# State space mixer of a two-layer diffusion backbone: where the decay masks are applied, and how the state products are formed

## The chip, the cores and the metric

One core of one Trainium2 chip runs the whole kernel. The metric is device microseconds of one execution, median over runs. TensorE (PE in the profile; its weight loads are PEld) multiplies matrices into PSUM, VectorE (DVE) and GpSimd (POOL) do elementwise work, ScalarE (ACT) does activations and copies, and DMA queues are issued from SyncE (SP) and from ScalarE. GpSimd does not touch PSUM in this kernel.

## The reference, cut to what matters

512 latent tokens and 256 context tokens of width 1024 go through two layers. Layer 0 is a gated linear attention mixer beside neighbourhood attention, layer 1 the state space mixer; after each comes a mixture of 16 experts. In layer 1 the context serves only as the start of the states. The mixer has 8 groups of 4 heads of 64 channels, a state of 128, and runs in both directions:

```python
def ssd_chunked(x, dt, a, bm, cm, h0):
    acum = jnp.cumsum(dtc * a, axis=2)
    seg = acum[:, :, :, None] - acum[:, :, None, :]
    decay = jnp.exp(jnp.where(causal, seg, -jnp.inf))
    cb = jnp.einsum('nblgk,nbsgk->nblsg', cc, bc)
    y_diag = jnp.einsum('nblsgh,nbsghp->nblghp', cb[..., None] * decay * dtc[:, :, None], xc)
    w_end = jnp.exp(acum[:, :, -1:] - acum) * dtc
    def step(hs, xs):
        y = y_d + jnp.einsum('blgk,bghpk->blghp', c_i, hs) * jnp.exp(a_i)[..., None]
        hs = exp(a_i[:, -1]) * hs + jnp.einsum('blgk,blghp->bghpk', b_i, x_i * w_i[..., None])
        return hs, y
```

The outputs of the two directions are added, then `dsk * x`, the gate silu(z), an RMS norm per group and the output projection follow. The kernel works with chunks of 128 positions instead of 64, which gives the same sums.

## The kernel before, in words

All of it is one function, `tile_backbone_kernel`. A scheduler takes the program in its written order, simulates it, and fixes for each engine and queue one order in which its instructions run; an engine that waits holds up all that stands behind it. So work of the next group is mixed into that of the present one on each engine.

The mixer starts at L1376. A first projection gives dt (64 rows: 2 directions by 32 heads). L1417 to L1476 make from it, per direction, the running sum of the decay `ac` within each chunk, `ad = ac - ln(dt)`, and the weights to a chunk's end; `ac` is stored to the DRAM tensor `acd`, and `ac`, `ad` and the weights are transposed on TensorE into `acT`, `adT` and `weT`.

Then a loop over the 8 groups (L1517). In one group: projections of x, B and C by `gemm_fm` (L825, float32 weights and inputs split into two parts, three matrix products each; `load_split` at L726 loads and splits, ScalarE casting and VectorE subtracting at L721, L722); a convolution of five taps on ScalarE and VectorE (L1482 to L1497, its running sum is `acc`); transpositions of x and B (L1545 to L1555, copied by ScalarE into `xk`, `bk`); C·B for four chunks in one PSUM bank of the `at` tag (L1556), which VectorE multiplies by a mask of ones and zeros per direction into `cb` (L1563); x weighted to the chunk's end on GpSimd (`xw`, L1572) and from it the states `st` of both directions, chunk by chunk (L1575 to L1597; GpSimd decays them, VectorE adds); the projection of z for the gate `zs` (L1598).

The part that changes is L1613 to L1651. It runs twice per group, for two halves `m` of 128 channels (two heads). A PSUM bank `o` is cleared. For each direction `d`, the two rows of `acd` are loaded on ScalarE's queue to all 128 partitions (`R`, 512 KB, two buffers). Eight VectorE instructions form `min(R, acT) - adT` in `mt` (L1627), ScalarE takes the exponential (L1629), VectorE multiplies by `cb[d]` (L1630). ScalarE takes the exponential of `R` itself (L1631) and GpSimd multiplies it by C (L1632). Then TensorE adds to the bank, per chunk and per head, x times `mt` (8 products with 64 columns of weights, 128 wide) and the chunk's state times `R` (again 8). Last, VectorE adds `dsk * x` and multiplies by the gate (L1646, L1648), ScalarE squares (L1649). The norm of a group (L1499: column sums, `rsqrt`, transposition, two products, a store to `yd`) is issued inside the next group's projections. In PSUM the tag `o` has one bank, `at` two, `tp` two and `mm` three.

After the loop, the output projection reads `yd` back (L1660), and the mixture of experts streams its weights.

The lines of the inner part that a sentence says badly:

```python
1618  for d in range(2):
1623      mt = sp.tile([128, 2, 4, 128], F32, name="mt", bufs=2)
1624      for hh in range(2):
1625          for c in range(4):
1626              h = col + hh
1627              V.tensor_scalar(mt[:, hh, c, :], R[:, hh, c, :], acT[:, c, h:h + 1], adT[:, c, h:h + 1],
1628                              op0=ALU.min, op1=ALU.subtract)
1635      def heads(c, w, r, last):
1636          for hh in range(2):
1637              mm(py[hh * 64:(hh + 1) * 64, c, :], w[:, hm][:, hh * 64:(hh + 1) * 64], r[:, hh, c, :], False, last)
1639      for c in range(4):
1640          heads(c, xk[:, c], mt, False)
1641      for n in range(4):
1642          heads(n if d == 0 else 3 - n, st[:, n, d], R, True)
```

In the trace each float32 matrix product shows as two TensorE instructions.

Of the kernel before, what the change touches and what calls it, by code (L numbers as in the profile page):

```python
# [10 lines left out]
F32 = mybir.dt.float32  # L11
# [11 lines left out]
LAT = 512  # L23
# [28 lines left out]
def kernel(ctx: ExitStack, tc: tile.TileContext, A: dict, out: bass.AP):  # L52
# [17 lines left out]
    def tp_bank(shape=None):  # L70
        return bank("tp", 2, shape)

    def at_bank(shape=None):
        return bank("at", 2, shape)

    def mm(o, l, r, start, stop, **k):
        return T.matmul(o, l, r, start=start, stop=stop, skip_group_check=True, **k)  # L77
# [1298 lines left out]
    with ExitStack() as mb:  # L1376
# [14 lines left out]
        acd = dram.tile([64, LAT], F32, name="acd")  # L1391
        lad = dram.tile([64, 4], F32, name="lad")
        with ExitStack() as sx:
            sp = sx.enter_context(tc.tile_pool(name="ssc", bufs=1, side="right"))
            tri = [sp.tile([128, 128], F32, name=f"stri{d}") for d in range(2)]
            for d in range(2):
                sgn = 1 - 2 * d
                G.memset(tri[d], 1.0)
                G.affine_select(out=tri[d], in_=tri[d], pattern=[[sgn, 128]], compare_op=ALU.is_ge, fill=0.0,
                                base=0, channel_multiplier=-sgn)  # L1400
# [7 lines left out]
            acT = sp.tile([128, NTL, 64], F32, name="acT")  # L1408
            adT = sp.tile([128, NTL, 64], F32, name="adT")
# [8 lines left out]
            e_ = sp.tile([64, TOK], F32, tag="mt", bufs=2, name="dte")  # L1418
            l_ = sp.tile([64, TOK], F32, tag="mt", bufs=2, name="dtl")
# [31 lines left out]
            V.tensor_tensor(ad, ac[:, :LAT], ad, ALU.subtract)  # L1451
# [16 lines left out]
            S.dma_start(out=acd[:, :], in_=ac[:, :LAT])  # L1468
            S.dma_start(out=eb.rearrange("p a b -> p (a b)"),
                        in_=lad.rearrange("a b -> (a b)").partition_broadcast(128))  # L1470
            S.activation(eb, eb, AF.Exp)
            for t, o, n in ((ac, acT, NTL), (ad, adT, NTL), (l_, weT, NT)):
                q = tp_bank([128, 8, 64])
                for i in range(n):
                    tr(q[:, i, :], t[:, i * 128:(i + 1) * 128])
                V.tensor_copy(o, q[:, :n, :])  # L1476
# [40 lines left out]
            for g in range(8):  # L1517
# [42 lines left out]
                cb = []  # L1560
                for d in range(2):
                    t = sp.tile([128, 4, 128], F32, name=f"cb{d}")
                    V.tensor_tensor(t, p, tri[d].unsqueeze(1).to_broadcast([128, 4, 128]), ALU.mult)  # L1563
                    cb.append(t)
# [48 lines left out]
                for m in range(2):  # L1613
                    py = bank("o", 1, [128, 4, 128])
                    clear(py)
                    hm = slice(m * 128, (m + 1) * 128)
                    for d in range(2):

                        col = d * 32 + g * 4 + m * 2
                        R = sp.tile([128, 2, 4, 128], F32, name="R", bufs=2)  # L1620
                        S.dma_start(out=R.rearrange("p h a b -> p (h a b)"),
                                    in_=acd[col:col + 2, :].rearrange("h t -> (h t)").partition_broadcast(128))
                        mt = sp.tile([128, 2, 4, 128], F32, name="mt", bufs=2)
                        for hh in range(2):
                            for c in range(4):
                                h = col + hh
                                V.tensor_scalar(mt[:, hh, c, :], R[:, hh, c, :], acT[:, c, h:h + 1], adT[:, c, h:h + 1],  # L1627
                                                op0=ALU.min, op1=ALU.subtract)
                        S.activation(mt, mt, AF.Exp)  # L1629
                        V.tensor_tensor(mt, mt, cb[d].unsqueeze(1).to_broadcast([128, 2, 4, 128]), ALU.mult)  # L1630
                        S.activation(R, R, AF.Exp)  # L1631
                        G.tensor_tensor(R, R, cT.rearrange("p (a b) -> p a b", a=4).unsqueeze(1).to_broadcast([128, 2, 4, 128]),  # L1632
                                        ALU.mult)

                        def heads(c, w, r, last):
                            for hh in range(2):
                                mm(py[hh * 64:(hh + 1) * 64, c, :], w[:, hm][:, hh * 64:(hh + 1) * 64], r[:, hh, c, :], False, last)

                        for c in range(4):
                            heads(c, xk[:, c], mt, False)  # L1640
                        for n in range(4):
                            heads(n if d == 0 else 3 - n, st[:, n, d], R, True)
                    y = sp.tile([128, LAT], F32, name="y", bufs=2)
                    sq = sp.tile([128, LAT], F32, name="ysq", bufs=2)
                    blk = g * 2 + m
                    V.scalar_tensor_tensor(y, xg[:, m, :LAT], vec("dsk", blk, 1), py.rearrange("p a b -> p (a b)"),  # L1646
                                           op0=ALU.mult, op1=ALU.add)
                    V.scalar_tensor_tensor(y, y, 0.5, zs[:, m, :], op0=ALU.mult, op1=ALU.mult)  # L1648
                    S.activation(sq, y, AF.Square)  # L1649
                    sqs.append(sq)  # L1650
                    ys.append(y)  # L1651
# [196 lines left out]
```

## Time and profile before

| | us |
|---|---|
| median of 3 runs | 2380.43 |
| lowest, highest | 2377.44, 2381.2 |
| the profiled execution, its own time | 2382.69 |
| its span, first to last instruction | 2381.0 |
| mixer's loop, from the first group's C·B product to the last group's | 1286.19 to 1753.08 |

The span is what the profile's views divide; 1.7 us of the execution lie around it. Busy time of TensorE counts overlapped instructions once, and their ends are modelled; distances between starts are the safer measure of what a stretch of matrix products costs. A group of instructions in the profile carries its line, engine, operation and tiles as output<-inputs. Matrix products are all issued in a helper at L77, so they are told apart by tiles: `o<-mt,xk` and `o<-R,st` are the heads, `at<-cT,bT` is C·B.

### The profile page before, as it was taken

The page shows a single profiled execution, that of the slowest core. Times are in us where ns is not written, and L with a number is a line of the kernel's source. Part 1 is how long each engine was busy: PE and PEld are TensorE (multiplying, and loading weights), DVE is VectorE, ACT ScalarE, POOL GpSimd, SP SyncE. Part 2 cuts the span into 40 slices and gives each one's busy share as a digit, 9 for nine tenths or more (in the row PEclk, how much of TensorE's full clock was granted, in tenths as well). Part 3 has the DMA queues.
Part 4 walks back from the last instruction along what each step waited for, and adds up shares of the span by engine and source line. Part 5 has one row for each costly group of instructions (what it writes and reads, how often), then busy time and mean ns, then how long its engine had stood idle before and what let it go on. Part 6 is the DMA issues. An engine that isn't in the chain of part 4 may idle for free. (4 is left out here: it accounts for less than half of the span.)

```text
span 2381.0 us, 37608 instructions
## 1 busy us (share of the span) xinstructions
PE 2228.0 (94%) x15522; PEld 1392.7 (58%) x15522; DVE 1273.3 (53%) x2231; ACT 847.0 (36%) x1408; POOL 513.9 (22%) x383
## 2 busy tenths in 40 slices
PE   7999999989999999999988999999989999988886
PEld 6888887877344444444476787777768633322222
DVE  5566476635243443343577888888885512222224
ACT  4446455522242343343463444434443211111111
POOL 1000044421121222221222434334442000000001
PEclk9999999999899999999998999999999899999999
DMA  8554311249999999999733232322256999999996
GB/s 270 162 163 150 103 37 55 71 137 338 352 368 366 370 379 387 368 383 356 271 101 108 91 124 92 94 84 89 89 178 243 358 366 418 419 419 418 419 418 264
DMA packets 253707, 587.94 MB, mean 247 GB/s; under 512 B 14240, under 2 KB 129056, under 8 KB 253536
## 3 DMA queue, kind: packets, MB, share of 16 engines
q1 hardware_dynamic: 240960, 548.44, 61.2%
q0 software_dynamic: 5280, 18.88, 3.1%
q10 hardware_dynamic: 7296, 18.22, 2.3%
q8 instruction: 122, 2.00, 0.3%
q14 instruction: 49, 0.40, 0.1%
HBM read 560.99 MB, written 24.51 MB: 246 GB/s over the span
## 5 line engine op out<-in xcount | busy, mean ns | idle before, releaser
L77 PE MATMUL mm<-w_moe,xs 128*32 128x512 f32 (+1 forms) x4080 | 596.3, 597 | 20.7 <-DMA w_moe<-in_w_dram 20.7
L77 PE MATMUL mm<-xh,w_s 128*128 128x512 f32 (+2 forms) x1824 | 479.1, 357 | 4.4 <-ACT z L1087 3.7
L77 PEld LDWEIGHTS mm<-w_moe,xs 128*32 128x32 f32 (+1 forms) x4080 | 171.1, 116 | 397.9 <-issue 336.4
L77 PEld LDWEIGHTS mm<-xh,w_s 128*128 128x128 f32 (+1 forms) x1824 | 307.3, 189 | 55.9 <-issue 8.2
L77 PE MATMUL mm<-xl,w_s 128*128 128x512 f32 (+1 forms) x912 | 296.4, 357 | 0.0
L77 PEld LDWEIGHTS mm<-xl,w_s 128*128 128x128 f32 x912 | 160.0, 189 | 24.7 <-issue 4.2
L77 PE MATMUL at<-w_s,hT_h 128*96 128x512 f32 x480 | 162.8, 405 | 1.6 <-POOL w_s L514 1.1
L514 DVE TENSOR_TENSOR w_s<-w_moe,w_s 128x1024 fp32r<-128x1024 f32 x90 | 126.9, 1432 | 62.9 <-ACT w_s L513 62.6
L1492 DVE SCALAR_TENSOR_TENSOR acc<-u,cwh,acc 128x770 f32<-128x770 f32 (+1 forms) x128 | 149.2, 1173 | 15.2 <-ACT acc L1489 13.9
L514 POOL TENSOR_TENSOR w_s<-w_moe,w_s 128x1024 fp32r<-128x1024 f32 x30 | 75.0, 2499 | 334.1 <-ACT w_s L513 257.7
L513 ACT CAST w_s<-w_moe 128x1024 fp32r<-128x1024 f32 x120 | 124.4, 1049 | 46.7 <-PE at L77 22.1
L1632 POOL TENSOR_TENSOR R<-R,cT 128x1024 f32<-128x1024 f32 x32 | 101.3, 3179 | 132.2 <-ACT R L1631 109.6
L77 PE MATMUL at<-w_moe,o 128*64 128x512 f32 x512 | 119.9, 599 | 8.9 <-DMA w_moe<-in_w_dram 7.3
L479 DVE TENSOR_TENSOR ha<-mm,ha 128x512 f32<-128x512 f32 x16 | 11.1, 691 | 217.6 <-PE mm L77 216.9
L77 PEld LDWEIGHTS at<-w_s,hT_h 128*96 128x96 f32 x480 | 75.1, 161 | 59.3 <-issue 22.6
L478 ACT ACTIVATE ha<-mm 128x512 f32<-128x512 f32 x16 | 9.6, 597 | 260.1 <-PE mm L77 260.1
L772 DVE TENSOR_TENSOR w_s<-w_raw,w_s 128x1024 fp32r<-128x1024 f32 x56 | 75.7, 1357 | 46.3 <-ACT w_s L771 46.1
L77 PE MATMUL at<-w_s,hT_l 128*96 128x512 f32 x240 | 94.2, 392 | 0.0
L1572 POOL TENSOR_TENSOR xw<-xk,weT 128x256 f32<-128x256 f32 x80 | 72.3, 935 | 98.5 <-ACT xk L1550 98.5
L647 DVE TENSOR_TENSOR ha<-mm,ha 128x512 f32<-128x512 f32 x16 | 11.1, 691 | 147.7 <-PE mm L77 147.7
L77 PE MATMUL mm<-w_s,xh 128*128 128x256 f32 x480 | 89.2, 290 | 0.2
L646 ACT ACTIVATE ha<-mm 128x512 f32<-128x512 f32 x16 | 9.6, 597 | 223.6 <-PE mm L77 223.6
(463 smaller groups left out, 3680.1 us busy)
## 6 DMA issues: line engine op xcount, KB each, us to landing
w_moe<-in_w_dram SPq DMA_DIRECT2D x380, 1024.0 KB
w_ada<-in_ada_w_dram SPq DMA_DIRECT2D x34, 1024.0 KB
w_raw<-in_ssd_w_in_dram SPq DMA_DIRECT2D x16, 1024.0 KB
R<-acd ACTq DMA_DIRECT2D x32, 512.0 KB
spare<-in_ada_w_dram SPq DMA_DIRECT2D x14, 1024.0 KB
w_raw<-in_ab_w_in_dram SPq DMA_DIRECT2D x12, 1024.0 KB
w_raw<-in_ssd_w_in_dram SPq DMA_DIRECT2D x16, 512.0 KB
w_raw<-in_ssd_w_out_dram SPq DMA_DIRECT2D x8, 1024.0 KB
```

The lines of the kernel that those rows point to most:

```text
L77: return T.matmul(o, l, r, start=start, stop=stop, skip_group_check=True, **k)
L478: S.activation(ha, B[0], AF.Silu)
L479: V.tensor_tensor(ha, B[1], ha, ALU.mult)
L513: S.copy(wh, w2[:, kk, :])
L514: (G if k % 4 == 3 else V).tensor_tensor(wl, w2[:, kk, :], wh.bitcast(F32), ALU.subtract)
L646: S.activation(ha, B[0], AF.Silu)
L647: V.tensor_tensor(ha, B[1], ha, ALU.mult)
L772: V.tensor_tensor(wl, r, wh.bitcast(F32), ALU.subtract)
L1492: V.scalar_tensor_tensor(acc[:, :n], u[:, i:i + n], cwh[:, i * 32 + cblk:i * 32 + cblk + 1], acc[:, :n], op0=ALU.mult, op1=ALU.add)
L1572: G.tensor_tensor(xw[:, i, d, :].rearrange("p (h c) -> p h c", h=4), xk[:, i, :].rearrange("p (h c) -> p h c", h=4), we[:, i, d, :].unsque ...
L1632: G.tensor_tensor(R, R, cT.rearrange("p (a b) -> p a b", a=4).unsqueeze(1).to_broadcast([128, 2, 4, 128]), ALU.mult)
```

## The change

Masks become addends in the exponent: the two mask tiles hold 0 and -1e30 instead of 1 and 0. `acT` and the minimum disappear. VectorE adds the mask to `R` in one instruction per direction, in place, and eight ScalarE exponentials of 128x128 take `ln(dt) - ac` as per-partition bias (`adN`). The two directions' results are summed on VectorE, multiplied once by C·B (now one plain copy, made by ScalarE), and go once through x. The state products no longer use a decayed C: for both heads at once, 128 channels of the state multiply C itself into a bank of its own (`at` or `tp`), and VectorE scales the result by exp(ac), stored once in DRAM (`ead`) and loaded as `E` by two DMAs per direction and half, each to 64 partitions. GpSimd adds the two directions' scaled results and adds them to y.

```diff
+        ead = dram.tile([64, LAT], F32, name="ead")
-                G.memset(tri[d], 1.0)
-                G.affine_select(out=tri[d], in_=tri[d], pattern=[[sgn, 128]], compare_op=ALU.is_ge, fill=0.0,
+                G.memset(tri[d], 0.0)
+                G.affine_select(out=tri[d], in_=tri[d], pattern=[[sgn, 128]], compare_op=ALU.is_ge, fill=-1e30,
...
-            acT = sp.tile([128, NTL, 64], F32, name="acT")
-            adT = sp.tile([128, NTL, 64], F32, name="adT")
+            adN = sp.tile([128, NTL, 64], F32, name="adN")
...
-            e_ = sp.tile([64, TOK], F32, tag="mt", bufs=2, name="dte")
-            l_ = sp.tile([64, TOK], F32, tag="mt", bufs=2, name="dtl")
+            e_ = sp.tile([64, TOK], F32, tag="R", bufs=3, name="dte")
+            l_ = sp.tile([64, TOK], F32, tag="R", bufs=3, name="dtl")
...
-            V.tensor_tensor(ad, ac[:, :LAT], ad, ALU.subtract)
+            V.tensor_tensor(ad, ad, ac[:, :LAT], ALU.subtract)
...
+            S.activation(msk[:, :LAT], ac[:, :LAT], AF.Exp)
+            S.dma_start(out=ead[:, :], in_=msk[:, :LAT])
...
-            for t, o, n in ((ac, acT, NTL), (ad, adT, NTL), (l_, weT, NT)):
+            for t, o, n in ((ad, adN, NTL), (l_, weT, NT)):
...
-                cb = []
-                for d in range(2):
-                    t = sp.tile([128, 4, 128], F32, name=f"cb{d}")
-                    V.tensor_tensor(t, p, tri[d].unsqueeze(1).to_broadcast([128, 4, 128]), ALU.mult)
-                    cb.append(t)
+                cb = sp.tile([128, 4, 128], F32, name="cb")
+                S.copy(cb, p)
...
+                    def heads(c, w, r, last):
+                        for hh in range(2):
+                            mm(py[hh * 64:(hh + 1) * 64, c, :], w[:, hm][:, hh * 64:(hh + 1) * 64], r[:, hh, c, :], False, last)
+                    Es = []
                     for d in range(2):
+                        h = d * 32 + g * 4 + m * 2
+                        E = sp.tile([128, 4, 128], F32, name="E", bufs=3)
+                        for hh in range(2):
+                            S.dma_start(out=E[hh * 64:(hh + 1) * 64].rearrange("p a b -> p (a b)"),
+                                        in_=ead[h + hh, :].partition_broadcast(64))
+                        q = at_bank([128, 4, 128]) if d == 0 else tp_bank([128, 4, 128])
+                        for n in range(4):
+                            c = n if d == 0 else 3 - n
+                            mm(q[:, c, :], st[:, n, d, hm], cT[:, c * 128:(c + 1) * 128], True, True)
+                        V.tensor_tensor(E, q, E, ALU.mult)
+                        Es.append(E)
+                    G.tensor_tensor(Es[0], Es[0], Es[1], ALU.add)
+                    mts = []
+                    for d in range(2):
                         col = d * 32 + g * 4 + m * 2
-                        R = sp.tile([128, 2, 4, 128], F32, name="R", bufs=2)
+                        R = sp.tile([128, 2, 4, 128], F32, name="R", bufs=3)
                         S.dma_start(out=R.rearrange("p h a b -> p (h a b)"),
                                     in_=acd[col:col + 2, :].rearrange("h t -> (h t)").partition_broadcast(128))
-                        mt = sp.tile([128, 2, 4, 128], F32, name="mt", bufs=2)
+                        mt = R
+                        V.tensor_tensor(mt, R, tri[d][:, None, None, :].to_broadcast([128, 2, 4, 128]), ALU.add)
                         for hh in range(2):
                             for c in range(4):
-                                h = col + hh
-                                V.tensor_scalar(mt[:, hh, c, :], R[:, hh, c, :], acT[:, c, h:h + 1], adT[:, c, h:h + 1],
-                                                op0=ALU.min, op1=ALU.subtract)
-                        S.activation(mt, mt, AF.Exp)
-                        V.tensor_tensor(mt, mt, cb[d].unsqueeze(1).to_broadcast([128, 2, 4, 128]), ALU.mult)
-                        S.activation(R, R, AF.Exp)
-                        G.tensor_tensor(R, R, cT.rearrange("p (a b) -> p a b", a=4).unsqueeze(1).to_broadcast([128, 2, 4, 128]),
-                                        ALU.mult)
...
-                        for c in range(4):
-                            heads(c, xk[:, c], mt, False)
-                        for n in range(4):
-                            heads(n if d == 0 else 3 - n, st[:, n, d], R, True)
+                                S.activation(mt[:, hh, c, :], mt[:, hh, c, :], AF.Exp, bias=adN[:, c, col + hh:col + hh + 1])
+                        mts.append(mt)
+                    V.tensor_tensor(mts[0], mts[0], mts[1], ALU.add)
+                    V.tensor_tensor(mts[0], mts[0], cb.unsqueeze(1).to_broadcast([128, 2, 4, 128]), ALU.mult)
+                    for c in range(4):
+                        heads(c, xk[:, c], mts[0], True)
...
+                    G.tensor_tensor(y, y, Es[0].rearrange("p a b -> p (a b)"), ALU.add)
```

## Rows read from the trace of the kernel before

**Rows 1.** The page, busy time of an engine, its share of the span, its instructions.

```profile
PE 2228.0 (94%) x15522; PEld 1392.7 (58%) x15522; DVE 1273.3 (53%) x2231; ACT 847.0 (36%) x1408; POOL 513.9 (22%) x383
```

**Rows 2.** Busy us (instructions) by stretch, seven groups of the mixer, their sum.

```profile
sum 466.89, PE 443.74 PEld 354.91 DVE 395.29 ACT 201.30 POOL 196.28; mean PE 63.39 PEld 50.70 DVE 56.47 ACT 28.76 POOL 28.04
```

**Rows 3.** Whom TensorE waited for, same seven groups: us in total, times, longest us.

```profile
PE o L77 <- DVE mt L1630: 7.1, 3, 3.0
PE at L1509 <- DVE rs_y L143: 6.7, 5, 2.1
PE at L77 <- DVE y L1512: 2.8, 2, 2.5
PE o L77 <- POOL R L1632: 2.4, 4, 1.2
```

**Rows 4.** The chain of waits over 1286 to 1760 us, shares by line.

```profile
by line: DVE acc L1492 18.0%; PE mm L77 12.8%; DVE mt L1627 12.1%; PE at L77 9.4%; DVE w_s L722 5.3%; DMA R<-acd 4.7%; POOL xw L1572 4.3%; DVE mt L1630 4.0%; PE o L77 3.9%; issue 3.6%; DMA w_raw<-in_ssd_w_in_dram 2.3%; DVE xg L1497 1.8%; AC
```

**Rows 5.** The table by stretch, after the mixer: PE, PEld, DVE, ACT, POOL, PEclk, DMA, GB/s.

```profile
1900.00:2381.00 481.00, 423.81 (x1862) 142.07 (x1861) 119.53 (x206) 60.81 (x111) 12.47 (x14) 0.99 0.96 391
```

**Rows 6.** TensorE's timeline, a pair of head stretches: start, us, instruction.

```profile
1526.69 1.09 PE L77 MATMUL o<-mt,xk 128*64 128x128 f32 x16
1527.61 1.04 PE L77 MATMUL o<-R,st 128*64 128x128 f32 x16
1528.59 0.96 PE L77 MATMUL mm<-xh,w_s 128*128 128x512 f32 x4
```

**Rows 7.** TensorE's timeline, a product of C and B.

```profile
1624.01 1.16 PE L77 MATMUL at<-cT,bT 128*128 128x128 f32 x8
1624.92 0.36 PE L77 MATMUL mm<-xh,w_s 128*128 128x256 f32 x1
```

**Rows 8.** Groups of instructions by line, VectorE, the seven groups: busy us, mean ns.

```profile
L1627 DVE TENSOR_SCALAR mt<-R,acT,adT 128x128 f32<-128x128 f32 x224 | 71.1, 389 | 4.9 <-DMA R<-acd 4.8
...
L1630 DVE TENSOR_TENSOR mt<-mt,cb 128x1024 f32<-128x1024 f32 x28 | 43.9, 1588 | 0.4 <-ACT mt L1629 0.4
...
L1563 DVE TENSOR_TENSOR cb<-at,stri 128x512 f32<-128x512 f32 x14 | 9.0, 681 | 3.5 <-PE at L77 3.5
```

**Rows 9.** The tile mt: duration ns min/median/max, first and last start us.

```profile
L1630 DVE TENSOR_TENSOR mt<-mt,cb x32: 1207/1216/3372, 1289.5 to 1787.0; 128x1024 f32<-128x1024 f32 x32
```

**Rows 10.** VectorE's timeline, two sets of eight mask exponents.

```profile
1515.64 2.14 DVE L1627 TENSOR_SCALAR mt<-R,acT,adT 128x128 f32<-128x128 f32 x8 [0.36 <-DMA R<-acd]
...
1519.23 4.23 DVE L1627 TENSOR_SCALAR mt<-R,acT,adT 128x128 f32<-128x128 f32 x8
```

**Rows 11.** GpSimd's timeline over the second of these.

```profile
1519.90 2.45 POOL L1632 TENSOR_TENSOR R<-R,cT 128x1024 f32<-128x1024 f32 x1 [12.31 <-ACT R L1631]
```

**Rows 12.** Groups of instructions by line, ScalarE, the seven groups.

```profile
L1629 ACT ACTIVATE mt<-mt 128x1024 f32<-128x1024 f32 x28 | 29.7, 1060 | 21.9 <-DVE mt L1627 21.7
L1631 ACT ACTIVATE R<-R 128x1024 f32<-128x1024 f32 x28 | 29.3, 1045 | 0.0
L1489 ACT ACTIVATE acc<-u,cbh,cwh 128x770 f32<-128x770 f32 x21 | 21.6, 1031 | 0.4
...
L1489 ACT ACTIVATE acc<-u,cbh,cwh 128x512 f32<-128x512 f32 x7 | 5.8, 824 | 0.0
...
L169 ACT COPY ada_row<-tp 128x128 f32<-128x128 f32 x4 | 1.1, 266 | 3.6 <-PE tp L77 3.6
```

**Rows 13.** The tensor acd: duration ns min/median/max of the issues of R's loads.

```profile
L1621 ACTq DMA_DIRECT2D R<-acd x32: 321/326/446, 1256.0 to 1774.2; - x32
```

**Rows 14.** Groups of instructions by line, GpSimd, the seven groups.

```profile
L1632 POOL TENSOR_TENSOR R<-R,cT 128x1024 f32<-128x1024 f32 x28 | 87.8, 3150 | 118.0 <-ACT R L1631 97.5 <-DVE cT L1497 10.5 <-PE at L1509 4.3
L1572 POOL TENSOR_TENSOR xw<-xk,weT 128x256 f32<-128x256 f32 x70 | 65.4, 965 | 55.8 <-ACT xk L1550 55.8
```

**Rows 15.** The chain of waits, a load of R: start, us from issue.

```profile
1511.93 3.69 DMA R<-acd
```

**Rows 16.** Whom VectorE waited for, the seven groups: us in total, times, longest us.

```profile
DVE mt L1627 <- DMA R<-acd: 4.8, 7, 1.7
```

More of the change, by code (lines that the diff above doesn't have):

```diff
@@ L1631 @@
-                        S.activation(R, R, AF.Exp)
-                        G.tensor_tensor(R, R, cT.rearrange("p (a b) -> p a b", a=4).unsqueeze(1).to_broadcast([128, 2, 4, 128]),
-                                        ALU.mult)
-                        def heads(c, w, r, last):
-                            for hh in range(2):
-                                mm(py[hh * 64:(hh + 1) * 64, c, :], w[:, hm][:, hh * 64:(hh + 1) * 64], r[:, hh, c, :], False, last)
-                        for c in range(4):
-                            heads(c, xk[:, c], mt, False)
```

## The prediction, made before the changed kernel was run

> **What bounds the kernel now.** I read the page first: of 2381.0 us TensorE is busy 94% [rows 1]. The change touches one stage, the state space mixer, so the next view is the table of busy time by stretch. Seven of its eight groups lie between the C·B product of the first group and that of the last, 466.89 us, 66.7 us a group [rows 2]. There TensorE is busy 443.74 us (95%), VectorE 395.29 us (85%), ScalarE 43%, GpSimd 42%: TensorE is nearly full and VectorE is the one behind it. The list of waits says whom TensorE waits for in its 23 us of idleness: VectorE's mask product 7.1 us, the norm's rsqrt 6.7, the last group's scaled rows 2.8, all three VectorE; GpSimd's product of decays and C 2.4 [rows 3]. The chain of waits over the same stretch runs through VectorE more than through TensorE: the convolution 18.0%, the mask exponents 12.1%, the mask product 4.0% [rows 4]. So an instruction taken off either engine should shorten a group, while one taken off ScalarE or GpSimd should not by itself. What follows the mixer, 481 us with the DMA engines 96% busy [rows 5], starts its steady weight stream when the mixer's buffers come free; I let it move with the mixer's end, one for one.
>
> **TensorE.** The two directions' masked matrices are now added before the product, so each of the 16 passes (8 groups, 2 halves) has one stretch of 16 instructions on x where it had two. One takes 1527.61 - 1526.69 = 0.92 us [rows 6]: 16 x 0.92 = 14.7 us gone. The state products change form: 8 products of 64 channels in 16 instructions, 1528.59 - 1527.61 = 0.98 us [rows 6], become 4 products of 128 channels in 8 instructions. That halves the instructions, but not the time: the C·B product has exactly that shape (4 products 128 by 128 in float32, 8 instructions) and takes 1624.92 - 1624.01 = 0.91 us [rows 7], so a pair of 64-channel products costs what one of 128 channels does. 32 x (0.98 - 0.91) = 2.2 us. TensorE loses 16.9 us in all. Bounds: each new product might run as cheaply as two of the old instructions, 0.49 us, which would give 15.7 us more; or, at half the granted clock, twice 0.91, which would cost 29 us. I take 0.91, the same shape in the same stage.
>
> **VectorE.** What goes, over seven groups: mask exponents 71.1 us, mask products 43.9, masked C·B 9.0 [rows 8]: 124.0 us, 17.7 a group. What comes per group: 8 additions or products of 128x1024 (4 masks, 2 sums, 2 products with C·B) and 4 products of 128x512 with one operand in PSUM. The first kind is the old mask product, median 1.216, mean 1.588 us, up to 3.372 [rows 8, 9]; the second is the old masked C·B, 0.68. What stretches the first kind is GpSimd: eight mask exponents take 2.14 us by themselves and 4.23 beside a GpSimd product [rows 10, 11]. That makes 12.4 to 15.4 us: a saving of 2.3 to 5.3 us a group, 18 to 42 in eight. I lean to the larger half, as GpSimd has less to do.
>
> A rule speaks against this exchange. Eight old exponent instructions take 2.14 us [rows 10], one new mask addition 1.216: by the rows the exchange wins. By the Trainium skill, "VectorE: DVE Perf Modes", the section on mode 2x_2P, a float32 tensor_scalar in SBUF may stream two elements a cycle and a tensor_tensor only one; by streaming alone the eight would take some 0.53 us and the addition 1.07 (estimates from that page), and VectorE would gain work. The row decides against it: the cost of eight starts outweighs the rate.
>
> **ScalarE.** Two exponentials of 128x1024 per mask, 59.0 us in seven groups [rows 12], 8.4 a group, become 32 of 128x128 with a per-partition bias, and a copy of C·B (0.6 us) joins. No row has this shape. From below, the 128x128 copy without such an operand, 0.266 us; from above, the convolution's activation with two such operands, 0.824 at 512 columns, less 384 columns at (1.031 - 0.824)/258 = 0.80 ns, 0.52 us [rows 12]. I take the middle, 0.39, for one operand: 32 x 0.39 + 0.6 = 13.1 us, 4.7 more a group (between 0.7 and 8.8). DMA issues on its queue rise from 4 to 12 a group at 0.326 us [rows 13]: 2.6 more. ScalarE goes from 28.8 to about 36 of 64 us: still slack, so no term; the price appears only as a wait (third rival). By the Trainium skill, "ScalarE: Activation LUTs", the section What ACT_TABLE_LOAD costs, such an instruction takes about 0.39 us and overlaps its neighbour by 0.09, so the 32 would take some 9.5 us (estimate from that page); no run here shows it yet, and the sum stays.
>
> **GpSimd.** Four products of 128x1024 at 3.150 us go; four additions of 128x512 come, between 0.965 (256 columns) and 3.150 [rows 14], by the line between them 1.7: 5.8 us less a group. Its busy time ends nothing now; what counts is the 2.4 us for which TensorE waited on it [rows 3], 2.7 in eight groups, which goes with its cause. The addition to y stands between two VectorE instructions: y comes about 2 us later, and behind the addition on GpSimd stand the next group's weighted copies of x. Both are used only during the next group's projections, whose matrix work covers them: nothing. In the last group, which has no successor, the output projection's earlier blocks cover them.
>
> **Loads.** R stays as it is, with a third buffer. New are 8 loads of 128 KB a group. An R load of 512 KB lands 3.69 us after its issue, and VectorE waited 4.8 us for all 28 [rows 15, 16]. If each of the new loads is as late as the worst R, 1.7 us; if it is early, 0. I take 0: the state products need neither R nor an exponential, so there is time. In the stage's first lines one transposition goes and one exponential and one store come, before a wait for the decays' own store; without that cover they cost one activation, under 0.82 us [rows 12].
>
> **Sum.** TensorE 16.9, the GpSimd wait 2.7, and of the norm's and the scaled rows' waits (6.7 + 2.8, 10.9 in eight groups) half, 5.4, because VectorE comes to them earlier. The mask product's own wait I leave: it is late today with one direction's chain before it, and now has both. 16.9 + 2.7 + 5.4 = 25.0. The profiled execution took 2382.7, 2.3 above the median of 2380.4 and 1.5 above the dearest of the three runs: 2357.7 by its measure; I say 2357.
>
> **Rivals.**
> First, *VectorE sets the pace throughout*. The chain [rows 4] speaks for it. All waits of TensorE on VectorE (16.6 in seven groups, 19.0 in eight) then go beside the 16.9 and 2.7: 38.6 us, 2344. Against it: the mask product's chain gets longer.
> Second, *TensorE's saving turns into waiting*. Before, a head could start after one direction's exponentials; now both masks, 16 small exponentials, a sum and a product must be over: 2 x 1.2 + 16 x 0.39 + 2 x 1.2 = 11 us of chain before the first of 16 instructions. If the scheduled order underrates that chain by 1.5 us a pass, 24 us of the 25 are eaten: 2381, no change. About 0.2% (4.8 us) is what a measurement of this kernel can tell from no change.
> Third, on the other side, *the loads of decay rows come late*. VectorE takes its instructions in order, and the 32 products with E wait for loads queued on ScalarE behind exponentials, with three buffers, where the fourth load of a group waits until y of the first half is summed. Behind a load that waits for its buffer stand, on ScalarE, the casts of the next weights and the emptying of TensorE's banks; behind a product that waits stands, on VectorE, the convolution. At the worst wait of today, 1.7 us each [rows 16], that is 54 us; VectorE's idle 10.2 us a group [rows 2] hide some of it, I say a third: 36 - 25 = 11 us slower, 2394. It decides above 25/32 = 0.8 us a load on the path. Against it: R, loaded in the same way, cost 4.8 us for 28.
> That the change does not do what it says is possible in one part: wider state products halve instructions and not time. That is in the sum.
>
> **Chances.** The forecast 0.62, its own range 2347 to 2370; VectorE alone 0.12; the eaten saving 0.11; late loads 0.15. Faster 0.74, same 0.11, slower 0.15. For 8 in 10 the range takes the first rival whole, down to 2338 for the better end of VectorE's bounds, and the second up to 2382; the late loads are left out.
>
> **What would show it.** After: TensorE instructions on mt halved, each stretch still 0.92; the state products in stretches of 8 at about 0.91; VectorE at 51 to 54 us a group, ScalarE 33; a group of 63 us; no wait of TensorE on GpSimd. Wrong if a state stretch takes well over 1 us, if VectorE waits on loads of E, or if TensorE's wait on the mask product passes 25 us.

## The result, and the profile after

The changed kernel takes 2350.99 us, median of 4 runs (2346.11 to 2351.55), beside 2380.0 for the kernel before on the same chip (4 runs, 2377.44 to 2381.2): a ratio of 0.9872, 95% interval 0.9858 to 0.9886. It is faster by 29 us; the forecast was 25 from its own profiled execution, 2357. The profiled execution took 2350.5 us, its span is 2348.8.

The page, the row that answers to [rows 1]:

```profile
PE 2196.0 (93%) x15006; PEld 1381.7 (59%) x15006; DVE 1224.8 (52%) x2022; ACT 865.4 (37%) x1609; POOL 471.8 (20%) x383
```

The gain is where the change is. The first warming product after the mixer starts at 1849.80 us where it started at 1881.66: 31.9 us earlier, of a span that is 32.2 shorter. What follows the mixer moved with its end, one for one, as the forecast let it. Inside the mixer the gain is uneven. The table by stretch, seven groups from C·B to C·B, answers to [rows 2]; its columns are PE, PEld, DVE, ACT and POOL busy us with instructions, then the granted clock, the DMA share and GB/s. Before:

```profile
1286.19:1355.10 68.91, 65.23 (x441) 52.30 (x441) 54.88 (x87) 28.95 (x43) 27.30 (x21) 0.97 0.36 115
1355.10:1424.80 69.70, 67.55 (x488) 54.39 (x488) 58.80 (x90) 31.07 (x46) 27.33 (x21) 1.00 0.35 114
1424.80:1489.40 64.60, 62.14 (x429) 48.96 (x429) 52.67 (x84) 27.40 (x41) 30.45 (x21) 1.00 0.32 99
1489.40:1558.20 68.80, 63.51 (x402) 50.41 (x403) 58.69 (x86) 29.77 (x47) 30.46 (x22) 0.97 0.27 85
1558.20:1624.01 65.81, 62.25 (x406) 50.22 (x405) 55.04 (x85) 27.16 (x39) 25.11 (x21) 0.98 0.27 88
1624.01:1688.80 64.79, 61.37 (x404) 49.17 (x403) 57.64 (x85) 28.61 (x43) 26.86 (x21) 1.00 0.29 90
1688.80:1753.08 64.28, 61.69 (x404) 49.45 (x404) 57.57 (x85) 28.34 (x43) 28.77 (x21) 1.00 0.30 95
```

After:

```profile
1287.16:1364.78 77.62, 68.04 (x406) 55.31 (x407) 50.35 (x61) 33.89 (x76) 21.75 (x21) 0.87 0.39 122
1364.78:1434.70 69.92, 64.38 (x410) 53.19 (x409) 53.05 (x63) 33.74 (x71) 22.42 (x21) 0.93 0.40 128
1434.70:1496.45 61.75, 61.75 (x384) 51.19 (x383) 48.81 (x61) 30.26 (x67) 22.24 (x21) 1.00 0.41 128
1496.45:1557.44 60.99, 60.12 (x351) 49.92 (x351) 50.95 (x61) 32.93 (x71) 23.03 (x21) 1.00 0.35 113
1557.44:1612.36 54.92, 54.92 (x320) 45.40 (x321) 47.46 (x57) 28.85 (x65) 20.45 (x18) 1.00 0.35 116
1612.36:1673.20 60.84, 59.68 (x346) 48.61 (x345) 50.54 (x59) 29.77 (x67) 22.38 (x22) 1.00 0.35 113
1673.20:1731.87 58.67, 57.59 (x342) 48.01 (x340) 50.99 (x60) 29.07 (x60) 26.21 (x25) 1.00 0.37 122
sum 444.71, PE 426.48 PEld 351.63 DVE 352.15 ACT 218.52 POOL 158.49; mean PE 60.93 PEld 50.23 DVE 50.31 ACT 31.22 POOL 22.64
```

So the last five groups went from 328.3 to 297.2 us (59.4 a group), and the first two from 138.6 to 147.5. The sum, -22.2, hides a gain of 31.1 and a loss of 8.9; the eighth group with the output projection gave another 10.7, and the stage's start lost 1.0.

TensorE's idle time tells the two parts apart. By the two tables (length less busy time) it was 5.8 us in the first two groups and 17.3 in the last five, most of it what [rows 3] list; now it is 15.1 and 3.1. After, the list of waits of the first two groups (whom TensorE waited for: us in total, times, longest):

```profile
PE at L77 <- DVE cT L1499: 6.7, 1, 6.7
PE tp L77 <- DVE modT L176: 3.8, 2, 2.1
PE tp L77 <- ACT ada_row L169: 3.4, 2, 1.7
PE mm L77 <- ACT w_s L721: 2.7, 1, 2.7
PE tp L77 <- DVE E L1631: 2.4, 2, 1.7
PE tp L77 <- DVE st L1596: 2.2, 2, 1.2
...
PE at L77 <- DVE cT L1499: 2.0, 2, 1.1
PE tp L88 <- DVE bT L1499: 1.1, 1, 1.1
```

The last two lines are the whole list for the last five groups: 3.1 us. The waits on the mask product, the norm's rsqrt, the scaled rows and GpSimd are all gone. The first line, 6.7 us, is the wait that ends at 1287.16 with the first group's C·B: it lies in the stage's start and not in the 15.1 us. Of the 15.1, 9.6 (`modT`, `ada_row`, `E`) stand in front of units that compute the next modulation vectors: four of them lie in these two groups (three before), one in the third, none in the groups behind. A unit needs a bank of `tp`, where half of the state products now lie. TensorE's timeline in the first group:

```profile
1305.33 1.08 PE L77 MATMUL tp<-w_ada,sT 128*32 128x128 f32 x32 [0.73 <-DVE E L1631]
1308.14 0.39 PE L77 MATMUL tp<-sel,ada_row 128*128 128x4 f32 x2 [1.72 <-ACT ada_row L169]
1310.21 1.93 PE L77 MATMUL tp<-w_ada,sT 128*32 128x128 f32 x32 [1.69 <-DVE modT L176]
1314.83 1.01 PE L77 MATMUL mm<-xh,w_s 128*128 128x512 f32 x2 [2.69 <-ACT w_s L721]
```

A unit starts when the product with E has emptied its bank (`E`), then waits for ScalarE's copy, then the next unit waits for VectorE to empty a bank again. What that costs beyond the waits is in the table by stretch, in steps of 6 us:

```profile
1299.00:1305.00 6.00, 3.42 (x25) 2.83 (x24) 5.13 (x8) 4.80 (x16) 0.62 (x1) 1.00 0.23 75
1305.00:1311.00 6.00, 2.25 (x50) 1.85 (x54) 2.77 (x5) 1.25 (x5) 2.54 (x2) 0.92 0.77 251
1311.00:1317.00 6.00, 3.31 (x30) 2.52 (x23) 2.99 (x3) 4.24 (x11) 2.19 (x1) 0.50 1.02 272
1317.00:1323.00 6.00, 5.44 (x18) 4.58 (x18) 5.17 (x5) 1.58 (x2) 2.14 (x1) 0.50 0.42 114
1323.00:1329.00 6.00, 6.00 (x33) 5.24 (x33) 1.23 (x1) 1.54 (x6) 0.00 (x0) 0.94 0.65 240
```

TensorE is busy 5.67 of the first 12 us; then the granted clock stands at 0.50, 1.2 GHz instead of 2.4, until after 1323. In the two rows at 0.50 TensorE is busy 8.75 us, with products that take about twice their time: one of 512 columns starts 0.42 us after another there (1316.28, 1316.70), and 0.23 at full clock (1520.22, 1520.45). The second group has the same picture from 1377 on.

The chain of waits, 1287 to 1739 us, answers to [rows 4]:

```profile
by line: PE mm L77 49.0%; PE at L77 12.1%; DVE acc L1494 7.0%; PE o L77 3.9%; DVE w_s L722 3.3%; DMA E<-ead 2.9%; issue 2.8%; PE tp L77 2.4%; DMA yin<-yd 2.4%; PE tp L88 2.1%; DMA R<-acd 1.8%; DVE E L1631 1.5%; DVE xg L1499 1.3%; DVE R L164
```

It was led by VectorE's convolution; now TensorE's projections are half of it.

Last, the groups of instructions by line, the seven groups, which answer to [rows 8, 12, 14]; busy us, mean ns, then the idle time before them:

```profile
L1645 ACT ACTIVATE R<-R,adN 128x128 f32<-128x128 f32 x224 | 69.0, 389 | 68.0 <-DVE R L1641 66.2 <-DVE w_s L722 1.8
L1641 DVE TENSOR_TENSOR R<-R,stri 128x1024 f32<-128x1024 f32 x28 | 37.7, 1347 | 23.6 <-DMA R<-acd 23.6
L1647 DVE TENSOR_TENSOR R<-R 128x1024 f32<-128x1024 f32 x14 | 19.2, 1372 | 0.7 <-ACT R L1645 0.7
L1648 DVE TENSOR_TENSOR R<-R,cb 128x1024 f32<-128x1024 f32 x14 | 17.6, 1296 | 4.6 <-ACT cb L1563 4.5
L1631 DVE TENSOR_TENSOR E<-at,E 128x512 f32<-128x512 f32 x14 | 9.6, 684 | 3.8 <-PE at L77 3.8
L1631 DVE TENSOR_TENSOR E<-tp,E 128x512 f32<-128x512 f32 x14 | 9.6, 683 | 7.3 <-DMA E<-ead 7.3
L1656 POOL TENSOR_TENSOR y<-y,E 128x512 f32<-128x512 f32 x14 | 26.8, 1915 | 1.1
L1633 POOL TENSOR_TENSOR E<-E 128x512 f32<-128x512 f32 x14 | 24.3, 1737 | 72.4 <-DVE E L1631 67.1 <-DMA E<-ead 5.3
```

### The profile page after: what moved, and what is told of

The parts are those of the page before. It is cut to its first block, busy times and chain, and to the rows that moved or that the text cites. A ratio compares the mean times of both kernels' runs of the same rounds, so it can differ in the third digit from the quotient of the medians.

```text
span 2348.8 us, 36706 instructions
## 1 busy us (share of the span) xinstructions
PE 2196.0 (93%) x15006; PEld 1381.7 (59%) x15006; DVE 1224.8 (52%) x2022; ACT 865.4 (37%) x1609; POOL 471.8 (20%) x383
## 5 line engine op out<-in xcount | busy, mean ns | idle before, releaser
L1494 DVE SCALAR_TENSOR_TENSOR acc<-u,cwh,acc 128x770 f32<-128x770 f32 (+1 forms) x128 | 137.9, 1082 | 15.3 <-ACT acc L1491 14.0
L513 ACT CAST w_s<-w_moe 128x1024 fp32r<-128x1024 f32 x120 | 124.4, 1049 | 47.6 <-PE at L77 22.2
L77 PEld LDWEIGHTS at<-w_s,hT_h 128*96 128x96 f32 x480 | 75.1, 161 | 59.4 <-issue 22.6
L1645 ACT ACTIVATE R<-R,adN 128x128 f32<-128x128 f32 x256 | 78.8, 389 | 69.9 <-DVE R L1641 68.1
```

Source lines behind the costliest of these rows:

```text
L513: S.copy(wh, w2[:, kk, :])
L1494: V.scalar_tensor_tensor(acc[:, :n], u[:, i:i + n], cwh[:, i * 32 + cblk:i * 32 + cblk + 1], acc[:, :n], op0=ALU.mult, op1=ALU.add)
L1645: S.activation(mt[:, hh, c, :], mt[:, hh, c, :], AF.Exp, bias=adN[:, c, col + hh:col + hh + 1])
```

## The experiments

Three questions: which half of the change pays, what the forecast's terms are worth one by one, and what causes the loss in the first two groups. A ratio is to the kernel before on the same chip (its medians there lie between 2379.85 and 2381.47 us), and "on after" means the difference to 2351.0.

**The halves.** The mask half alone, on the kernel before: masks as addends, eight exponentials with a bias, the directions summed, one product with C·B, one stretch of heads; the decayed C and the 64-channel state products stay.

```diff
-V.tensor_scalar(mt[:, hh, c, :], R[:, hh, c, :], acT[...], adT[...], op0=ALU.min, op1=ALU.subtract)   # x8
-S.activation(mt, mt, AF.Exp)
-V.tensor_tensor(mt, mt, cb[d]..., ALU.mult)
+V.tensor_tensor(mt, R, tri[d]..., ALU.add)
+S.activation(mt[:, hh, c, :], mt[:, hh, c, :], AF.Exp, bias=adN[...])   # x8
 S.activation(R, R, AF.Exp); G.tensor_tensor(R, R, cT..., ALU.mult)
+V.tensor_tensor(mts[0], mts[0], mts[1], ALU.add)
+V.tensor_tensor(mts[0], mts[0], cb..., ALU.mult)
```

> The mask half of the change by itself: masks added in the exponent, one sum and one product for both directions, one head stretch per pass; the states still multiply the decayed C (exponential of R, product on GpSimd, 64 channels at a time), no E. TensorE loses 14.7 us, VectorE 17.7 - 8 x 1.36 = 6.8 us a group (8 new instructions at the 1.36 us that they take in the changed kernel), ScalarE gains more than in the whole change, as it keeps the exponential of R. Theory T (TensorE's own work paces the mixer): 2380 - 15 = 2365, between 2360 and 2370. Rival V (VectorE paces it): more than the whole change brought, as the whole change adds four products with E: 2351 or less. Rival S (the gain came from the state half): no change, 2375 to 2380.

Measured: 2384.61 us, 1.002 (1.0005 to 1.0035). The 2365 that the forecast's terms give is missed; no change (rival S) is nearest. TensorE's heads did get 15.4 us shorter (65.5 to 50.1, by distances between starts), and the mixer ended 4.8 us later all the same. TensorE's waits in the mixer rose from 45.6 to 54.2 us, which is 8.6 of the 20.2 us that this leaves to explain. The rest lies in TensorE's own instructions, beside a granted clock that was 0.95 on average over the mixer, and 0.97 before. The list of waits, 1280 to 1760 us:

```profile
PE at L1508 <- DVE rs_y L143: 9.8, 2, 6.1
PE at L77 <- ACT ysq L1645: 6.6, 3, 3.0
```

Both wait for the end of a half: its square, its norm. ScalarE is the engine that grew, from 295.3 to 343.0 busy us in the mixer, as it has the exponentials of `R` besides.

The state half alone: masks, two products with C·B and two stretches of heads as before, computed in place in `R` with three buffers.

```diff
-S.activation(R, R, AF.Exp)
-G.tensor_tensor(R, R, cT..., ALU.mult)
-heads(n if d == 0 else 3 - n, st[:, n, d], R, True)   # x4
+mm(q[:, c, :], st[:, n, d, hm], cT[:, c * 128:(c + 1) * 128], True, True)   # x4
+V.tensor_tensor(E, q, E, ALU.mult)
+G.tensor_tensor(Es[0], Es[0], Es[1], ALU.add); G.tensor_tensor(y, y, Es[0], ALU.add)
```

> The state half by itself: 128 channels of the state multiply C, results scaled by loaded rows E, GpSimd adds; masks as before (eight minimum-and-subtract instructions per direction, in place in R with three buffers, two products with C.B, two head stretches a pass). TensorE loses 2.2 us, GpSimd 5.8 us a group, VectorE gains 4 x 0.68 = 2.7 us a group. T: 2380 - 2.2 - 2.7 (the waits on GpSimd) = 2375, between 2370 and 2380. V: 8 x 2.7 = 22 us slower, 2402. S: most of the gain, 2355 to 2360.

Measured: 2367.62 us, 0.9929 (0.9905 to 0.9952): 14 us faster on its own, where its TensorE and GpSimd terms in the forecast came to 5; it lies between the ranges of T and S, and V is out. So the half that takes almost nothing off TensorE pays, and the half that takes 14.7 us off it does not. Apart, the two come to some 10 us, together to 29: nearly 20 us are there only when both are.

**The forecast's terms.** The heads twice, in the changed kernel:

```diff
-V.tensor_tensor(mts[0], mts[0], mts[1], ALU.add)
-V.tensor_tensor(mts[0], mts[0], cb..., ALU.mult)
-heads(c, xk[:, c], mts[0], True)
+V.tensor_tensor(mts[d], mts[d], cb..., ALU.mult)   # d = 0, 1
+heads(c, xk[:, c], mts[d], d == 1)                 # d = 0, 1
```

> The changed kernel, but the two directions' masks are not summed: each is multiplied by C.B and goes through x by itself. VectorE has the same number of instructions of the same size (two products instead of a sum and a product), TensorE gets back 16 x 0.92 = 14.7 us. T: 2351 + 14.7 = 2366, between 2361 and 2370. V: 2351, no change from the changed kernel.

Measured: 2363.01 us, 0.9928 (0.9907 to 0.9948): 12.0 on after, near the 14.7 of the forecast's term, and V is out. With the state half in place the saving of TensorE is worth most of its face value.

The sum alone, on the kernel before: everything as it was, but both directions' masked matrices added before one stretch of heads.

```diff
 V.tensor_tensor(mt, mt, cb[d]..., ALU.mult)
-heads(c, xk[:, c], mt, False)
+V.tensor_tensor(mts[0], mts[0], mts[1], ALU.add)   # after both directions
+heads(c, xk[:, c], mts[0], True)
```

> The kernel before with one edit: the two directions' masked matrices (minimum, subtraction, one large exponential and the product with the masked C.B of each direction, all as before) are summed and go through x once. TensorE loses 14.7 us, VectorE gains 2 x 1.5 = 3 us a group, ScalarE and GpSimd are as before. It asks why the mask half alone brought nothing. Theory A (ScalarE, with 32 small exponentials and still the exponential of R, ate the saving there): without them the saving shows, 2380 - 10 = 2370, between 2362 and 2372. Theory J (the join of both directions before the first head ate it): nothing again, 2378 to 2386. Theory D (VectorE, with 24 us more, eats it): 2380 to 2395.

Measured: 2404.5 us, 1.0093 (1.0071 to 1.0114): the same 16 stretches off TensorE, and 23 us slower, beyond the ranges of all three theories. Its list of TensorE's waits, 1280 to 1780 us:

```profile
PE o L77 <- DVE mt L1643: 9.2, 6, 4.1
PE at L1509 <- DVE rs_y L143: 9.0, 2, 5.6
PE tp L88 <- DVE bT L1497: 9.0, 3, 4.7
PE o L77 <- POOL R L1638: 7.3, 4, 2.6
```

L1643 is the added sum, L1638 GpSimd's product of decays and C. TensorE's waits in the mixer are 72.5 us here, 27 more than before, and the granted clock over it is 0.94 where it was 0.97. So the saving does turn into waiting, as the forecast's second rival had it. But the heads' own waits, on the sum and on GpSimd's product, are 16.5 us where they were 9.5 [rows 3], 7 of the 27. The others stand elsewhere, and VectorE has 24 us more to do in this kernel; which share the join has and which VectorE's load is not separated.

The mask addition done twice in the changed kernel (the masked places then get -2e30): 43 us of VectorE's time more, nothing else.

```diff
-V.tensor_tensor(mt, R, tri[d]..., ALU.add)
+V.tensor_tensor(mt, R, tri[d]..., ALU.add)   # x2
```

> The changed kernel with each mask added twice (the exponent of what is masked out is -2e30 instead of -1e30, the rest is the same): VectorE gets 4 x 1.35 = 5.4 us more a group, 43 us in all, which takes it from 50 to 56 us a group, what it had before; TensorE's work is unchanged. T: VectorE fits beside TensorE's 60 us, a few more waits: 2351 to 2361. V: 43 us slower, 2394.

Measured: 2358.85 us, 0.99 (0.9879 to 0.9921), 8 on after. The kernel takes 19% of what VectorE is given: VectorE does not set the pace in the changed kernel, and the first rival falls.

State products as twice 64 channels, in the changed kernel:

```diff
-mm(q[:, c, :], st[:, n, d, hm], cT[...], True, True)
+mm(q[hh * 64:(hh + 1) * 64, c, :], st[:, n, d, hm][:, hh * 64:(hh + 1) * 64], cT[...], True, True)   # hh = 0, 1
```

> The changed kernel with each state product of 128 channels made as two of 64 (16 instructions a stretch instead of 8, the form of before). By the rows of before a stretch costs 0.98 instead of 0.91 us: 32 x 0.07 = 2.2 us slower, 2351 to 2355. Rival (the number of instructions is what costs): a stretch of 16 costs twice one of 8, 29 us slower, 2380.

Measured: 2354.8 us, 0.9884 (0.9864 to 0.9905), 4 on after with overlapping runs (2347.54 to 2358.19), so not told from no change. The wider form is worth little, as forecast.

GpSimd's work given back: in the changed kernel two products of 128x1024 per pass whose result nobody reads.

```diff
 V.tensor_tensor(mts[0], mts[0], cb..., ALU.mult)
+G.tensor_tensor(mts[1], mts[1], cT..., ALU.mult)   # x2
```

> The changed kernel with GpSimd's four products of 128x1024 a group given back, as work whose result nobody reads (two per pass on the second mask buffer, after the sum): 12.6 us more on GpSimd a group, TensorE, VectorE and ScalarE have the instructions of the changed kernel. It asks what in the state half pays. Theory G (GpSimd's reading slows VectorE, and its queue delays the norm and the states): 8 us or more slower, 2359 or more. Theory W (what pays is that TensorE no longer waits in order for a product behind ScalarE and GpSimd, not GpSimd's load): 2350 to 2355.

Measured: 2395.38 us, 1.006 (1.0044 to 1.0077): 44 us on after, as theory G has it and far beyond its 8. An engine that is busy 22.6 of 63.5 us a group costs that when it is given 12.6 us more. Two things are seen. First, VectorE's instructions with both inputs in SBUF are stretched where they run beside GpSimd's: the product with C·B (L1648), which always does here, takes 2777 ns on average where it took 1296, and the mask addition (L1641), which mostly does not, 1363 where it took 1347. VectorE's timeline:

```profile
1508.50 2.79 DVE L722 TENSOR_TENSOR w_s<-w_raw,w_s 128x1024 fp32r<-128x1024 f32 x1
1511.21 3.41 DVE L1648 TENSOR_TENSOR R<-R,cb 128x1024 f32<-128x1024 f32 x1
```

and GpSimd's beside it:

```profile
1506.92 6.62 POOL L1650 TENSOR_TENSOR R<-R,cT 128x1024 f32<-128x1024 f32 x2 [3.14 <-DVE cT L1499]
```

The products with E, one input in PSUM, kept their 684 ns. Second, the dead products hold a buffer of `R`, so the next load of `R` waits for them, and ScalarE's queue behind that load. The list of waits has it:

```profile
ACT st L1578 <- POOL R L1650: 26.2, 6, 6.6
```

The kernel before had the same coupling: its `R` too was free only after GpSimd's product and the heads that read it. How the 44 us divide between the two is open; a kernel with the dead products on a buffer of their own was not tried.

**What still costs time in the changed kernel.** Both state products in banks of `at`, none in `tp`:

```diff
-q = at_bank([128, 4, 128]) if d == 0 else tp_bank([128, 4, 128])
+q = at_bank([128, 4, 128])
```

> The changed kernel with both directions' state products in the two at banks, so that tp holds only transpositions and the modulation units. Theory P (the modulation units of the first two groups wait for tp banks that hold state products, 8 us): 2344 to 2349. Rival: the at banks, which the norm and the states also use, become the wait: 2351 to 2360.

Measured: 2336.92 us, 0.9818 (0.98 to 0.9837), 14 us below after, twice the largest gain that was expected. The first two groups in its table by stretch:

```profile
1288.98:1353.77 64.79, 61.86 (x346) 51.60 (x343) 49.49 (x60) 32.06 (x74) 24.91 (x21) 0.94 0.39 127
1353.77:1416.15 62.38, 62.38 (x416) 51.35 (x415) 51.97 (x63) 34.20 (x74) 20.76 (x21) 1.00 0.43 144
```

127.2 us where the changed kernel takes 147.5, and TensorE waits 2.9 us in them instead of 15.1. No wait on a modulation unit is left in them. The new tag also moved the units: two of the four now run before the first C·B, in the stage's start, which gets 1.8 us longer, so the start and the two groups together end some 18.5 us earlier (1416.15 for 1434.70). That the tag costs 14 us is shown; how much of it is the wait for a bank and how much the place of the units is not separated.

The loads of `E` on SyncE's queue:

```diff
-S.dma_start(out=E[hh * 64:(hh + 1) * 64]..., in_=ead[h + hh, :].partition_broadcast(64))
+SY.dma_start(out=E[hh * 64:(hh + 1) * 64]..., in_=ead[h + hh, :].partition_broadcast(64))
```

> The changed kernel with the loads of E issued from SyncE's queue instead of ScalarE's. Theory Q (the first group's loss, 8 us of TensorE idleness more than before, comes from ScalarE standing behind E's issues until the rows have been stored): 6 to 8 us faster, 2343 to 2346. Rival: SyncE's queue holds the weight loads behind the E loads: 2351 or slower.

Measured: 2345.43 us, 0.9858 (0.9836 to 0.988), 6 below after. By itself this is not clear of noise (after: 0.9858 to 0.9886); the same step on top of the bank tag, below, is. What went is in ScalarE's waits of the changed kernel, in the seven groups:

```profile
ACT w_s L721 <- issue: 7.5, 2, 4.5
ACT ada_row L169 <- issue: 5.0, 2, 2.7
```

These 12.5 us, in which ScalarE does nothing but issue loads of its own, are not in the lists of the runs with `E` on SyncE's queue, and not in that of the kernel before. One of them in ScalarE's timeline:

```profile
1306.67 1.11 ACTq L1625 DMA_DIRECT2D E<-ead  x2
1307.82 0.27 ACT L169 COPY ada_row<-tp 128x128 f32<-128x128 f32 x1 [2.72 <-issue]
```

The copy of a modulation unit stands behind two issues, and TensorE, at 1308.14 above, behind the copy.

Both together, and then the stage's four small stores and its load of the chunk decays on SyncE's queue as well:

```diff
-S.dma_start(out=lad[...]) / acd[...] / ead[...] / eb
+SY.dma_start(out=lad[...]) / acd[...] / ead[...] / eb
```

> The changed kernel with both better placements: state products of both directions in the at banks, loads of E on SyncE's queue. If the two gains (14 and 6 us) come from different waits they add: 2351 - 20 = 2331. If both removed the same wait of the first groups: 2337, as with the banks alone.

> The same, and the stage's four small stores and the load of the chunk decays also on SyncE's queue, so that ScalarE stands behind none of them at the start. TensorE's wait of 7.6 us for the copy of x in the first group goes if ScalarE's queue made it: 5 us faster than with E on SyncE alone, 2326 to 2331. Rival (ScalarE waits for the loaded decays all the same, in its exponential of them): no change against it.

Measured: 2330.03 us, 0.9778 (0.9755 to 0.9801), and 2330.18, 0.9782 (0.9757 to 0.9807). The two gains add to within 1 us (14.1 + 5.6 would give 2331.3), as two separate causes would. With the banks of `at` in place, moving `E` brings 6.9 us, and all runs of the one (2327.24 to 2333.97) lie below all of the other (2334.09 to 2339.21). The second kernel is no faster than the first: the rival of its forecast holds, and the five transfers of the stage's start cost nothing on ScalarE's queue. These two are the fastest kernels of this study, 51 us below the kernel before.

Two buffers of `R` instead of three, in the changed kernel:

```diff
-R = sp.tile([128, 2, 4, 128], F32, name="R", bufs=3)
+R = sp.tile([128, 2, 4, 128], F32, name="R", bufs=2)
```

> The changed kernel with two buffers for R instead of three (as many as before; the mask chain works in place in them). Theory B (the third buffer is what makes the two halves worth more together than apart: with two, the next pass cannot load its rows until both directions' masks of this pass have gone through x): TensorE waits on the mask product again, 2370 or more. Theory N (the buffer does not matter, removed work does): 2347 to 2355.

Measured: 2350.24 us, 0.9871 (0.985 to 0.9892). The third buffer is worth nothing here.

## Why the prediction was right, point by point

**TensorE, -16.9 us: right in the sum, and its two parts off by as much in opposite ways.** By distances between starts the heads and state products took 65.5 us in the mixer and now take 48.5: -17.0. A state stretch took about what the row of C·B said, 0.91; the first line here starts 0.89 us before the second:

```profile
1374.66 1.06 PE L77 MATMUL at<-cT,st 128*128 128x128 f32 x8
1375.55 0.46 PE L77 MATMUL tp<-cT,st 128*128 128x128 f32 x2
```

But all state products together fell from 34.8 to 29.9 us, 4.9 instead of 2.2, and the products on x from 30.7 to 18.6, 12.1 instead of 14.7: a stretch of 16 that nothing interrupts now takes 1.02 us (from 1373.09 to 1374.11, for one), not "still 0.92", and half of them are interrupted. That the two misses cancel is luck. One bound beside them is miscounted: at 0.49 us a stretch the gain over the 0.91 that was taken is 13.4 us, not 15.7.

**That this term is paid out: right here, not in general.** The forecast put it at face value and gave the eaten saving 0.11. Put back, it costs 12.0 us; without the state half it is eaten (mask half alone) or worse (sum alone, +23). So there is a condition that the forecast did not have: the state half must go with it. A likely reason is that the engines before the joined heads must not also hold ScalarE's exponentials of `R` and GpSimd's products, which the state half removes; this is argued from the runs that kept both, and no run took out one of them alone.

**The waits, -8.1 us: the step that was mis-sized.** In the last five groups TensorE's idle time fell by 14.2 us (17.3 to 3.1), more than all that the forecast took; in the first two it rose by 9.3 (5.8 to 15.1), with the clock at half behind it. Over the whole mixer the waits went from 45.6 to 44.6 us: of the 8.1, one was gained in the sum. The forecast searched for new waits on the path of the mask and of E, and let the state products' banks pass without a price; the bank tag, one line of the diff, cost more than anything else in the changed kernel that a run took out. With `at` the kernel came out at 2336.92, below the forecast's own range. The rest of the 31.9 us, some 14, lies in instructions that did not change and in the gaps between them (projections 362.9 to 358.9 us, weighted x times B 38.7 to 36.1). It has signs of both kinds in it: the granted clock fell from 0.98 to 0.90 in the first two groups, and rose from 0.97 to 1.00 in the eighth and the output projection. A few matrix records are missing in each trace, so it is not divided further. The forecast named none of these 14 us; that they stand in for the waits and bring the time so near to 2357 is luck.

**GpSimd: right in the instructions, wrong in the sentence "its busy time ends nothing".** The additions took 1.74 and 1.92 us where 1.7 was taken, and the wait of 2.4 us went. But its products also stretched VectorE and held `R`, and the run that gave them back lost 44 us. That the state half alone gave 14 us instead of 5 fits this; the share of GpSimd in that was argued, not measured.

**VectorE: right in the lines that change.** They come to 93.7 us in seven groups against 124.0 [rows 8]: 4.3 a group, of 2.3 to 5.3. The whole engine came to 50.3 us a group, just below the 51 to 54. The exchange went as the rows said: a mask addition took 1.35 us where eight small instructions took 2.14 [rows 10]. By the streaming rates alone that the Trainium skill, "VectorE: DVE Perf Modes", section on mode 2x_2P, gives, VectorE would have gained work; the trace shows that they did not decide.

**ScalarE: the price of one right, their sum too high.** One exponential took 389 ns, but eight in a row took 2.45 us, so each after the first added 0.29, and the 32 cost 9.9 us a group (69.0 in seven) where 12.5 was summed; ScalarE came to 31.2 instead of 33. The Trainium skill, "ScalarE: Activation LUTs", section What ACT_TABLE_LOAD costs, had it nearer: 0.39 us with an overlap of 0.09 gave an estimate of 9.5, and the trace agrees.

**The loads.** Third rival: VectorE's wait on `E` came to 7.3 us and that on `R` rose from 4.8 [rows 16] to 23.6, with 13 us a group in which VectorE is idle (63.5 less 50.3); the mechanism is there, a loss from it is not seen. The forecast had named such a wait as a sign that it is wrong: the sign came, and the time did not follow it. An issue of `E`, taken at 0.326 us, took a median of 0.53 (0.45 to 1.66). The place where the rival did bite, ScalarE's queue, it named; the price was the 6 us of the run without it, and not 36.

## What to carry to other kernels

A saving on the busiest engine can turn into waiting: it did so twice where two chains were joined and nothing else was taken away. When a change joins two chains, look at whether the same change also empties the engines on the joined one, and test the halves apart. Read a new PSUM tile's tag like a queue: ask whose banks it takes, above all those of work that is interleaved only in some iterations, and look at the stage group by group, since a sum over groups hid a gain of 31 and a loss of 9 us. Ask what stands behind the issue of a load on an engine that also computes: moving the loads of `E` to a queue without such work won 6 us, moving five transfers of the stage's start nothing.

## What the runs showed of the hardware

A GpSimd product with two inputs in SBUF stretched a VectorE product of the same kind from 1.21 us up to 3.41, and left smaller ones with an input in PSUM at their 0.68. The Trainium skill, "GPSIMD Engine Reference", section Key points, states that the two engines contend where VectorE has two SBUF inputs; the trace agrees, and shows the size.

A stretch of waits was charged twice here: TensorE had been busy 5.67 us of 12 when its granted clock fell from 1.00 to 0.50 (2.4 to 1.2 GHz), and what came next ran at that rate, 0.42 us for a product that takes 0.23.

Two matrix products with 64 columns of weights cost about as much as one with 128 (0.98 us for a stretch of 16 instructions before, 0.89 for one of 8 after), and a broadcast load to 64 partitions took longer to issue (median 0.53 us) than one of four times its size to 128 (0.326).
